# A two-layer RG-LRU and sparse-attention trunk on one core: convolution taps ordered ahead of the scans, and compressed values held as 128-row tiles

## The chip, the core and the metric

One core of a Trainium2 chip runs the whole program. The metric is the device time of one execution in microseconds (us), lower is better. The kernel before takes 1337.06 us (median of 3 runs, 1336.85 to 1337.19).

## What is computed

The input x is 512 tokens by 1024 channels in float32. Layer 0 is an RG-LRU block and a gated FFN, layer 1 is sparse attention (NSA) and a second gated FFN. Every sub-layer starts with an RMSNorm and ends with a residual add, and the trunk ends with a norm. The two parts that the change touches, cut from the reference:

```python
def rglru_mixer(x, w_in, conv_w, conv_b, gate_w, gate_b, a_param, w_out):
    y_br, x_br = jnp.split(x @ w_in, 2, axis=-1)          # 1280 channels each
    y_br = jax.nn.gelu(y_br)
    xc = causal_dwconv(x_br, conv_w, conv_b)              # 4 taps over time
    g = jnp.einsum('bsnc,gncd->gbsnd', xb, gate_w)        # 10 blocks of 128 x 128, two gates
    r_gate, i_gate = sigmoid(g + gate_b)
    log_a = -8 * r_gate * softplus(-a_param)
    bterm = sqrt(-expm1(2 * log_a)) * i_gate * xc
    h = scan of h[t] = exp(log_a)[t] * h[t-1] + bterm[t]
    return (h * y_br) @ w_out
...
# nsa_mixer, for each of 4 kv groups (4 heads each) and each block of queries
    p_cmp = masked_softmax(q k_cmp^T - alibi) * mask      # 31 compressed keys
    o_cmp = p_cmp @ v_cmp
...
    o = gate0 * o_cmp + gate1 * o_sel + gate2 * o_win
```

## The kernel before

**Layout.** Activations stand transposed, channels on the 128 partitions and 512 tokens along the free axis. A product in float32 is made as three matmuls in the fp32r format (`mm3`, L213 to L215): weight high part by data high part, high by low, low by high. So each weight tile that a DMA brings (`wraw`) is split by `_split`: ScalarE (ACT) copies its high part (`whi`, L184) and VectorE (DVE) subtracts for the low part (`wlo`, L185). `w()` wraps these splits in `high_priority(offset=HP)`, HP being 100, two weight tiles ahead of their use.

**Who orders the work.** Outside the attention core a scheduler of the tile framework orders each engine's instructions, by the order in the code, shifted by priorities, and by its own estimates. Inside the attention core (`tc.manual_schedule()`) the order is that of a table of steps in the code (`at(step, engine, f)`), the same for both kernels.

**The recurrent block** (`lru`, L402 on). Ten channel blocks n of 128 are worked through one after the other. For each: `project` makes `py[n]` and `px[n]` on TensorE (PE); `conv(n)` evacuates `px` with the norm's factor (`xr`, L424, DVE), starts `xc` on ACT (L426), adds three taps on DVE (L429, 128x511, 128x510, 128x509), and splits the result into `ch` (ACT, L433) and `cl` (DVE, L434); `gate_mm(n)` makes the two gates on PE from `ch` and `cl`; `gate_act(n)` is ACT's sigmoids and a POOL multiply (L466). The recurrence is made two blocks at a time (`burst`): exponentials, roots and GELUs on ACT, then for each block `back1` (DVE L482 and L484, POOL L483), `back2` (DVE L487, the scan L488, and a POOL multiply L489) and `back3` (`hh` on ACT L494, `hl` on DVE L495). `yev` evacuates `py` (L420, DVE). The output projection then reads `hh` and `hl` as its data, in chunks of eight blocks and then the last two.

**The attention core.** Scores of a unit (group g, 128 queries i, branch) are made by PE (L987, L988), reduced on DVE into one of NP = 10 buffers `P` (L1000), exponentiated on ACT, scaled on POOL (L1017), transposed on PE (L1041), split into `ph` (ACT) and `sq` (DVE L1050), and multiplied with the values `V2` on PE (L1057, L1062). The compressed branch's probabilities of group g stand in one tile of 128 rows, 32 rows for each query block i. The last key tile of a unit adds them with two matmuls (L1061) that use 32 rows of the array:

```python
cs_ = slice(32 * i, 32 * i + 32)
for pc in Pc[g]:
    T.matmul(po, Vc[cs_, g], pc[cs_], start=False, stop=False)
```

`Vc` (128 x 4 x 128) holds the compressed values with the same rows repeated for the four query blocks. It is written once by ACT (L863) and DVE (L864).

Of the kernel before, what the change touches and what calls it, by code (L numbers as in the profile page):

```python
# [10 lines left out]
F32 = mybir.dt.float32  # L11
F32R = mybir.dt.float32r
AF = mybir.ActivationFunctionType
ALU = mybir.AluOpType
# [3 lines left out]
NT = 512  # L18
# [7 lines left out]
WARM = 10  # L26
WLO, QLO, KLO, OLO = True, 'G', 'V', 'V'
KG = 3
NP = 10


UNITS = ((3, (0,)), (3, (1,)), (0, (0, 1)), (2, (0,)), (2, (1,)), (1, (0,)), (1, (1,)))
# [29 lines left out]
    ("o", 7, 114.23, 120.26),  # L62
)
HP = 100

START = {1: (1, 0), 3: (0, 1), 4: (1, 1)}
KA, DEF = 8, 5
# [4 lines left out]
P_CW, P_CB, P_GB, P_AP = 40, 80, 90, 110  # L72
# [28 lines left out]
class Trunk:  # L101
# [301 lines left out]
    def lru(self):  # L403
        S, V, G, T, prm = self.S, self.V, self.G, self.T, self.prm
        with ExitStack() as s:
# [3 lines left out]
            col = lambda c: prm[:, c:c + 1]  # L409
            py, px, pg = {}, {}, {}  # L410
            y, xc, xcs, r, ig, u, sq = {}, {}, {}, {}, {}, {}, {}
# [8 lines left out]
                V.tensor_mul(y[n], py[n], self.rbc)  # L420

            def conv(n):
                xr = p.tile([128, NT], F32, name="xr")
                V.tensor_mul(xr, px[n], self.rbc)  # L424
                xc[n] = p.tile([128, NT], F32, name="xc", bufs=3)
                S.activation(xc[n], xr, AF.Identity, scale=col(P_CW + 30 + n), bias=col(P_CB + n))  # L426
                for k in (2, 1, 0):
                    d = 3 - k
                    V.scalar_tensor_tensor(xc[n][:, d:], xr[:, :NT - d], col(P_CW + 10 * k + n),  # L429
                                           xc[n][:, d:], op0=ALU.mult, op1=ALU.add)  # L430
                ch = p.tile([128, NT], F32R, name="ch")
                cl = p.tile([128, NT], F32R, name="cl")
                S.activation(ch, xc[n], AF.Copy)  # L433
                V.tensor_sub(cl, xc[n], ch.bitcast(F32))  # L434
                xcs[n] = (ch, cl)
# [48 lines left out]
                V.tensor_mul(ig[n], ig[n], sq[n])  # L484

            def back2(n):
                V.scalar_tensor_tensor(ig[n], r[n], 1.0, ig[n], op0=ALU.add, op1=ALU.mult)  # L487
                V.tensor_tensor_scan(u[n], r[n], ig[n], 0.0, op0=ALU.mult, op1=ALU.add)  # L488
                self.G.tensor_mul(u[n], u[n], y[n])  # L489

# [76 lines left out]
            po = {}  # L567
# [106 lines left out]
    def nsa(self):  # L674
        S, V, G, T, prm, cst = self.S, self.V, self.G, self.T, self.prm, self.cst
        tc, a = self.tc, self.a
        with ExitStack() as s:
            kp = s.enter_context(tc.tile_pool(name="nsa_k", bufs=1))
# [2 lines left out]
            K2l = [kp.tile([128, 2, NT], F32R, name=f"K2l{g}") for g in range(4)]  # L681
            V2 = kp.tile([128, 4, 2, 4, 128], F32R, name="V2")
            Kc = kp.tile([128, 4, 32], F32, name="Kc")
            Vc = kp.tile([128, 4, 128], F32R, name="Vc")
            gtok = kp.tile([128, 4, 48], F32, name="gtok")
            Q = {}

# [70 lines left out]
            first = [project()]  # L758
# [3 lines left out]
            for kv in range(2):  # L762
                for j in range(2):
# [4 lines left out]
                    for gg in range(2):  # L768
                        b = 64 * gg
                        for par in range(2):  # L770
                            ob = 64 * par
                            for hf in range(2):
                                src = tv[b:b + 64, par::2, hf:hf + 31]
                                pc = P_POS + 32 * kv + 16 * par + 8 * hf
# [16 lines left out]
            for c in range(4):  # L791
                hi, lo = self.w()
                for kk in range(2):
                    k = 2 * c + kk
# [65 lines left out]
                    T.matmul(pk[:, 64 * g:64 * g + 64], hv4[:, m, g].rearrange("p r c -> p (r c)"),  # L860
                             w2[:, 256 + 128 * m:256 + 128 * m + 64], start=(m == 0), stop=(m == 1))
            pkv = pk[:, :256].rearrange("p (g d) -> p g d", g=4)
            S.activation(Vc[:, :, :64], pkv, AF.Copy)  # L863
            V.tensor_sub(Vc[:, :, 64:], pkv, Vc[:, :, :64].bitcast(F32))  # L864
            q_tile(1)
            cs.close()

# [165 lines left out]
            def values(u, steps):  # L1033
                g, i, br = u
# [17 lines left out]
                def pv(kt):  # L1052
                    if br == 0 and kt == 0:
                        Po[g, i] = newO()
                    po = Po[g, i]
                    last = br == 1 and kt == i
                    T.matmul(po, V2[:, kt, br, g], st["h", kt], start=(br == 0 and kt == 0), stop=False)  # L1057
                    if last:
                        cs_ = slice(32 * i, 32 * i + 32)
                        for pc in Pc[g]:  # L1060
                            T.matmul(po, Vc[cs_, g], pc[cs_], start=False, stop=False)  # L1061
                    T.matmul(po, V2[:, kt, br, g], st["l", kt], start=False, stop=last)  # L1062

                for kt in range(i + 1):
# [182 lines left out]
```

## Time and profile before

| what | value |
|---|---|
| median of 3 runs | 1337.06 us (1336.85 to 1337.19) |
| the profiled execution's own time | 1337.11 us |
| its span, first to last instruction | 1335.3 us |
| PE busy | 1309.2 us (98%), 6174 records |
| DVE busy | 790.4 us (59%) |
| ACT busy | 609.8 us (46%) |
| POOL busy | 251.7 us (19%) |
| chain that ended last | PE 88%, DVE 6%, ACT 2%, issue 2% |

The span starts with the recurrent block (to about 190 us), then the first FFN (to about 610 us), the attention layer (to about 910 us, its core from about 700) and the second FFN. A busy share is an average over these stages: DVE is busy 61.88 of the 69.2 us from 80 to 149.2 us.

### The profile page before, as it was taken

Reading aid. Unit: us, or ns where it says so; the run is one execution under the profiler, and the core shown is the slowest. Engines: PE = TensorE matmul, PEld = TensorE weight load, DVE = VectorE, ACT = ScalarE, POOL = GpSimd, SP = SyncE. Lnnn points to the kernel's source line nnn. Section 1 sums busy time; section 2 is a strip of 40 time slices with the busy share of each in tenths; the row PEclk is TensorE's granted clock in tenths of the full one; section 3 lists DMA queues with packets and bytes.
Section 4 is the critical chain, followed back from the end, with each engine's and each line's share of the span. In section 5 each row is a group of like instructions: output and inputs, shape, how many; then the busy total and the mean of one; then the engine's idle time right before and its main releaser. Section 6 shows DMA issues by size and latency. Waiting matters only on the chain.

```text
span 1335.3 us, 16299 instructions
## 1 busy us (share of the span) xinstructions
PE 1309.2 (98%) x6174; PEld 1064.8 (80%) x6174; DVE 790.4 (59%) x1260; ACT 609.8 (46%) x977; POOL 251.7 (19%) x260
## 2 busy tenths in 40 slices
PE   9989999999999999999999999999999999999997
PEld 7877787888888888887787787778888888888886
DVE  8798766555555533336357978876655555552223
ACT  5778844333333322221348878875433333332220
POOL 2222232000000001115007567643000000000110
PEclk9999999999999999999999999999999999999998
DMA  7222222232222222223231011013222222222221
GB/s 239 87 71 89 78 95 80 99 104 98 95 95 95 95 95 95 95 79 134 101 111 32 19 46 33 17 33 113 93 95 99 100 101 95 95 95 95 95 79 64
DMA packets 36223, 117.72 MB, mean 88 GB/s; under 512 B 4144, under 2 KB 7728, under 8 KB 36144
## 3 DMA queue, kind: packets, MB, share of 16 engines
q1 hardware_dynamic: 34848, 115.61, 25.5%
q8 instruction: 48, 0.79, 0.2%
q10 hardware_dynamic: 1296, 1.07, 0.2%
q14 instruction: 31, 0.25, 0.1%
HBM read 114.57 MB, written 2.10 MB: 87 GB/s over the span
## 4 chain that ended last, share of the span: by engine, by line
PE 88%; DVE 6%; issue 2%; ACT 2%; DMA 0%; POOL 0%; SPq 0%; POOLq 0%; DVEq 0%; ACTq 0%
PE bank L214 25%; PE bank L213 25%; PE bank L215 25%; PE bank L1041 2%; PE bank L1062 2%; PE bank L1057 1%; PE bank L987 1%; PE bank L988 1%; PE bank L839 1%; ACT L226 1%; PE bank L1061 1%; PE bank L800 1%; DVE u L488 1%; PE bank L801 1%; DVE xl L254 1%
## 5 line engine op out<-in xcount | busy, mean ns | idle before, releaser
L184 ACT ACTIVATE whi<-wraw 128x1024 fp32r<-128x1024 f32 x144 | 151.8, 1055 | 330.5 <-PE bank L214 282.3
L214 PE MATMUL bank<-xl,whi 128*128 128x512 f32 (+1 forms) x768 | 299.8, 390 | 2.4 <-DVE xl L254 2.3
L213 PE MATMUL bank<-xh,whi 128*128 128x512 f32 (+1 forms) x768 | 300.5, 392 | 0.5 <-DVE qn L726 0.2
L215 PE MATMUL bank<-xh,wlo 128*128 128x512 f32 (+1 forms) x768 | 299.4, 390 | 1.0 <-DVE wlo L185 0.5
L185 DVE TENSOR_TENSOR wlo<-wraw,whi 128x1024 fp32r<-128x1024 f32 x132 | 162.7, 1233 | 141.6 <-ACT whi L184 131.2
L264 POOL TENSOR_TENSOR ssum<-ssum,sq 128x512 f32<-128x512 f32 x27 | 44.9, 1663 | 789.5 <-issue 581.1
L214 PEld LDWEIGHTS bank<-xl,whi 128*128 128x128 f32 (+1 forms) x768 | 143.7, 187 | 34.1 <-DVE xl L254 4.6
L215 PEld LDWEIGHTS bank<-xh,wlo 128*128 128x128 f32 (+1 forms) x768 | 143.6, 187 | 32.7 <-DVE wlo L185 1.0
L213 PEld LDWEIGHTS bank<-xh,whi 128*128 128x128 f32 (+1 forms) x768 | 143.8, 187 | 31.2 <-DVE X L911 0.7
L184 ACT ACTIVATE whix<-wrawx 128x1024 fp32r<-128x1024 f32 x57 | 60.4, 1059 | 131.7 <-PE bank L214 122.4
L214 PE MATMUL bank<-xl,whix 128*128 128x512 f32 x296 | 117.0, 395 | 0.0
L213 PE MATMUL bank<-xh,whix 128*128 128x512 f32 x296 | 116.7, 394 | 0.0
L215 PE MATMUL bank<-xh,wlox 128*128 128x512 f32 x296 | 115.4, 390 | 0.0
L213 PE MATMUL bank<-fh,whi 128*128 128x512 f32 (+1 forms) x272 | 104.0, 382 | 0.0
L214 PE MATMUL bank<-fl,whi 128*128 128x512 f32 (+1 forms) x272 | 103.9, 382 | 0.0
L215 PE MATMUL bank<-fh,wlo 128*128 128x512 f32 (+1 forms) x272 | 103.8, 382 | 0.0
L185 DVE TENSOR_TENSOR wlox<-wrawx,whix 128x1024 fp32r<-128x1024 f32 x57 | 71.9, 1261 | 39.4 <-ACT whix L184 39.3
L621 DVE TENSOR_TENSOR ar<-bank,rbc 128x512 f32<-128x512 f32 x48 | 33.2, 691 | 99.5 <-PE bank L215 99.5
L1017 POOL TENSOR_SCALAR P<-P,c,gtok 128x512 f32<-128x512 f32 (+3 forms) x128 | 79.3, 634 | 45.3 <-DVE c L1013 34.5
L631 DVE TENSOR_TENSOR b<-bank,rbc 128x512 f32<-128x512 f32 x48 | 33.2, 691 | 86.2 <-PE bank L215 86.2
L226 ACT ACTIVATE P<-P,nm 128x512 f32<-128x512 f32 (+3 forms) x128 | 70.9, 556 | 15.1 <-DVE nm L1000 13.6
L226 ACT ACTIVATE t<-t 128x512 f32<-128x512 f32 x48 | 30.4, 632 | 98.0 <-DVE t L627 98.0
(217 smaller groups left out, 2326.2 us busy)
## 6 DMA issues: line engine op xcount, KB each, us to landing
wraw<-in_ffn_in_dram SPq DMA_DIRECT2D x65, 512.0 KB, 3.3
wraw<-in_ffn_out_dram SPq DMA_DIRECT2D x32, 512.0 KB, 3.3
wrawx<-in_ffn_in_dram SPq DMA_DIRECT2D x31, 512.0 KB, 3.3
wrawx<-in_ffn_out_dram SPq DMA_DIRECT2D x16, 512.0 KB, 3.2
wraw<-in_nsa_in_dram SPq DMA_DIRECT2D x16, 512.0 KB, 3.2
wraw<-in_lru_in_dram SPq DMA_DIRECT2D x12, 512.0 KB, 3.6
w<-in_cmp_w_dram SPq DMA_DIRECT2D x8, 512.0 KB, 4.6
wraw<-in_nsa_out_dram SPq DMA_DIRECT2D x8, 512.0 KB, 3.3
```

The lines of the kernel that those rows point to most:

```text
L184: self.S.activation(hi[:, c], raw[:, c], AF.Copy)
L185: (self.G.tensor_sub if self.manual and WLO else self.V.tensor_sub)(lo[:, c], raw[:, c], hi[:, c].bitcast(F32))
L213: mm(ps, wh, xh, start=first, stop=False)
L214: mm(ps, wh, xl, start=False, stop=False)
L215: mm(ps, wl, xh, start=False, stop=last)
L226: ins = self.S.activation(out, in_, func, **k)
L264: self.sq_eng.tensor_add(self.ssum, self.ssum, sq)
L621: V.tensor_mul(ar, pa, self.rbc)
L631: V.tensor_mul(b, pb, self.rbc)
L1017: G.tensor_scalar(Ps[g, i, br][r], Ps[g, i, br][r], st["c"][:, br, r:r + 1], gtok[:, i, gc:gc + 1], op0=ALU.mult, op1=ALU.mult)
L1041: T.transpose(st["t", kt][:, 128 * r:128 * r + 128], Ps[u][r][:, 128 * kt:128 * kt + 128], self.ident)
L1062: T.matmul(po, V2[:, kt, br, g], st["l", kt], start=False, stop=last)
```

## The change

In the recurrent block `conv(n)` now runs at a priority raised by 150 (CHP; the weight splits have 100), and the instruction L487 of `back2`, which stands ahead of the scan L488, may not be placed on DVE ahead of the last tap that was recorded so far (`self.tap`). That is an order on one engine without a semaphore.

In the attention layer `Vc` becomes 128 x 4 x 4 x 128: for each query block i a tile of 128 rows in which only rows 32i to 32i+31 are filled. POOL sets it to zero first, ACT and DVE fill it with four instructions each in place of one, and the two matmuls use all 128 rows with the whole tile `pc`. The zero rows add nothing, so the sums are the same. NP goes from 10 to 9.

```diff
-NP = 10
+NP = 9
...
+CHP = 150
...
             def conv(n):
+                with self.tc.high_priority(offset=CHP):
+                    conv_ops(n)
+
+            def conv_ops(n):
                 xr = p.tile([128, NT], F32, name="xr")
...
                 for k in (2, 1, 0):
                     d = 3 - k
-                    V.scalar_tensor_tensor(xc[n][:, d:], xr[:, :NT - d], col(P_CW + 10 * k + n),
-                                           xc[n][:, d:], op0=ALU.mult, op1=ALU.add)
+                    tap = V.scalar_tensor_tensor(xc[n][:, d:], xr[:, :NT - d], col(P_CW + 10 * k + n),
+                                                 xc[n][:, d:], op0=ALU.mult, op1=ALU.add)
+                self.tap = getattr(tap, "ins", tap).name
...
             def back2(n):
-                V.scalar_tensor_tensor(ig[n], r[n], 1.0, ig[n], op0=ALU.add, op1=ALU.mult)
+                ins = V.scalar_tensor_tensor(ig[n], r[n], 1.0, ig[n], op0=ALU.add, op1=ALU.mult)
+                self.tc.add_manual_dep(getattr(ins, "ins", ins), self.tap, mybir.DependencyInfo(
+                    mybir.DependencyClass.NoSync, mybir.DependencyReason.DATA), reason="taps first")
                 V.tensor_tensor_scan(u[n], r[n], ig[n], 0.0, op0=ALU.mult, op1=ALU.add)
...
-            Vc = kp.tile([128, 4, 128], F32R, name="Vc")
+            Vc = kp.tile([128, 4, 4, 128], F32R, name="Vc")
+            G.memset(Vc.bitcast(F32), 0.0)
...
-            S.activation(Vc[:, :, :64], pkv, AF.Copy)
-            V.tensor_sub(Vc[:, :, 64:], pkv, Vc[:, :, :64].bitcast(F32))
+            for i in range(4):
+                rs = slice(32 * i, 32 * i + 32)
+                S.activation(Vc[rs, i, :, :64], pkv[rs], AF.Copy)
+                V.tensor_sub(Vc[rs, i, :, 64:], pkv[rs], Vc[rs, i, :, :64].bitcast(F32))
...
-                        cs_ = slice(32 * i, 32 * i + 32)
                         for pc in Pc[g]:
-                            T.matmul(po, Vc[cs_, g], pc[cs_], start=False, stop=False)
+                            T.matmul(po, Vc[:, i, g], pc, start=False, stop=False)
```

The lines of the changed kernel are up to 14 higher: L424 is L430, L429 is L435, L434 is L441, L487 and L488 are L494 and L498, L495 is L505, L184 and L185 are L185 and L186, L226 is L227.

**DVE in the recurrent block, block 5's convolution.** These are VectorE's instructions behind `xr` of block 5 up to its `cl`. `hl_642` and `hl_749` are the recurrence's decay of blocks 2 and 3, `hh_919` is `y` of block 6. Before:

```order
L185 TENSOR_TENSOR wlox<-wrawx,whix 128x1024
L487 SCALAR_TENSOR_TENSOR ig<-hl_642,ig 128x512
L484 TENSOR_TENSOR ig<-ig,sqr 128x512
L429 SCALAR_TENSOR_TENSOR xc<-xr,prm,xc 128x511
L488 SCALAR_TENSOR_TENSOR u<-hl_642,ig 128x512
L429 SCALAR_TENSOR_TENSOR xc<-xr,prm,xc 128x510
L487 SCALAR_TENSOR_TENSOR ig<-hl_749,ig 128x512
L429 SCALAR_TENSOR_TENSOR xc<-xr,prm,xc 128x509
L488 SCALAR_TENSOR_TENSOR u<-hl_749,ig 128x512
L420 TENSOR_TENSOR hh_919<-bank_820,rbc 128x512
L185 TENSOR_TENSOR wlo<-wraw,whi 128x1024
L434 TENSOR_TENSOR cl<-xc,ch 128x512
```

The same place in the changed kernel:

```order
L186 TENSOR_TENSOR wlox<-wrawx,whix 128x1024
L489 SCALAR_TENSOR_TENSOR u<-hl_749,u 128x512
L491 TENSOR_TENSOR ig<-ig,sqr 128x512
L435 SCALAR_TENSOR_TENSOR xc<-xr,prm,xc 128x511
L435 SCALAR_TENSOR_TENSOR xc<-xr,prm,xc 128x510
L435 SCALAR_TENSOR_TENSOR xc<-xr,prm,xc 128x509
L494 SCALAR_TENSOR_TENSOR ig<-hl_642,ig 128x512
L498 SCALAR_TENSOR_TENSOR u<-hl_642,ig 128x512
L421 TENSOR_TENSOR hh_919<-bank_820,rbc 128x512
L441 TENSOR_TENSOR cl<-xc,ch 128x512
```

The three taps now follow each other, one pair of L487 and scan stays between them and `cl`, the pair of block 3 has gone behind the next block's taps, and a weight split has gone behind `cl`. `xr` itself has moved ahead of `back1` of block 3, whose L482 (L489 now) stood ahead of it.

**ACT at the end of the recurrent block.** This is ScalarE from the last gate's sigmoid (`hl_1308`, block 9) to the roots (`sqr`) of the last burst; the exponentials are `hl_1271` and `hl_1308` from themselves. Before:

```order
L226 ACTIVATE hl_1308<-bank_1300,prm 128x512
L184 ACTIVATE whix<-wrawx 128x1024
L226 ACTIVATE ig<-bank_1304,prm 128x512
L226 ACTIVATE u<-hl_1308,sp 128x512
L226 ACT_TABLE_LOAD
L226 ACTIVATE hl_1271<-hl_1271,sp 128x512
L184 ACTIVATE whi<-wraw 128x1024
L226 ACTIVATE hl_1308<-hl_1308,sp 128x512
L226 ACT_TABLE_LOAD
L226 ACTIVATE sqr<-u 128x512 x2
L184 ACTIVATE whi<-wraw 128x1024
L226 ACT_TABLE_LOAD
```

In the changed kernel:

```order
L227 ACTIVATE hl_1308<-bank_1300,prm 128x512
L504 ACTIVATE hh_1296<-u 128x512
L227 ACTIVATE ig<-bank_1304,prm 128x512
L227 ACTIVATE u<-hl_1308,sp 128x512
L185 ACTIVATE whix<-wrawx 128x1024
L185 ACTIVATE whi<-wraw 128x1024
L227 ACT_TABLE_LOAD
L227 ACTIVATE hl_1271<-hl_1271,sp 128x512
L227 ACTIVATE hl_1308<-hl_1308,sp 128x512
L227 ACT_TABLE_LOAD
L227 ACTIVATE sqr<-u 128x512
L185 ACTIVATE whi<-wraw 128x1024
```

`hh` of block 7 (`hh_1296`) has moved in between the two gates' sigmoids, and a weight split now stands between the two roots, ahead of the second.

**POOL at the start of the attention layer.** `ssum` is the norm's sum over the residual that the first FFN leaves. In the changed kernel:

```order
L265 TENSOR_TENSOR ssum<-ssum,sq 128x512 x7
L279 TENSOR_TENSOR rtok<-nv,mhalf 128x4
L265 TENSOR_TENSOR ssum<-ssum,sq 128x512 x6
L696 MEMSET Vc 128x2048
L265 TENSOR_TENSOR ssum<-ssum,sq 128x512
L279 TENSOR_TENSOR rtok<-nv,mhalf 128x4
```

The zeroing stands ahead of the last of seven adds; before, the seven followed each other.

## Rows read from the trace of the kernel before

**Rows 1.** The first line of the page: the span.

```profile
span 1335.3 us, 16299 instructions
```

**Rows 2.** Who PE waited for over the whole span: us in total, number of waits, longest us. Two rows of twelve, the two largest.

```profile
PE bank L214 <- DVE cl L434: 4.7, 2, 3.0
PE bank L213 <- ACT ch L433: 3.7, 2, 2.6
```

**Rows 3.** Stretches of the span: its length, then the busy time (and instructions, those that reach in counted) of PE, PEld, DVE, ACT and POOL, the mean granted TensorE clock, DMA share and GB/s.

```profile
80.00:149.20 69.20, 63.25 (x266) 50.55 (x265) 61.88 (x73) 57.60 (x76) 19.19 (x16) 0.98 0.25 82
95.80:104.70 8.90, 4.82 (x13) 3.27 (x12) 8.86 (x13) 6.82 (x10) 1.61 (x2) 0.81 0.24 74
127.00:129.70 2.70, 0.97 (x5) 0.49 (x3) 2.70 (x4) 2.27 (x3) 0.38 (x1) 1.00 0.11 23
149.20:156.00 6.80, 4.17 (x11) 2.71 (x10) 6.39 (x6) 2.75 (x4) 2.64 (x2) 0.75 0.01 4
700.00:905.00 205.00, 201.66 (x1187) 155.96 (x1188) 166.24 (x490) 163.28 (x413) 131.54 (x171) 1.00 0.09 31
```

**Rows 4.** DVE in order of time around block 5's convolution: start us, length us, line, operation, tiles, shapes.

```profile
86.57 1.10 DVE L482 SCALAR_TENSOR_TENSOR u<-hl,u 128x512 f32<-128x512 f32 x1
87.59 0.68 DVE L424 TENSOR_TENSOR xr<-bank,rbc 128x512 f32<-128x512 f32 x1
...
89.37 0.68 DVE L487 SCALAR_TENSOR_TENSOR ig<-hl,ig 128x512 f32<-128x512 f32 x1
...
90.57 1.77 DVE L429 SCALAR_TENSOR_TENSOR xc<-xr,prm,xc 128x511 f32<-128x511 f32 x1
92.27 1.21 DVE L488 TENSOR_TENSOR_SCAN u<-hl,ig 128x512 f32<-128x512 f32 x1
93.40 0.72 DVE L429 SCALAR_TENSOR_TENSOR xc<-xr,prm,xc 128x510 f32<-128x510 f32 x1
94.05 1.78 DVE L487 SCALAR_TENSOR_TENSOR ig<-hl,ig 128x512 f32<-128x512 f32 x1
95.75 0.74 DVE L429 SCALAR_TENSOR_TENSOR xc<-xr,prm,xc 128x509 f32<-128x509 f32 x1
96.41 1.21 DVE L488 TENSOR_TENSOR_SCAN u<-hl,ig 128x512 f32<-128x512 f32 x1
...
98.13 1.98 DVE L185 TENSOR_TENSOR wlo<-wraw,whi 128x1024 fp32r<-128x1024 f32 x1
100.03 0.68 DVE L434 TENSOR_TENSOR cl<-xc,ch 128x512 fp32r<-128x512 f32 x1
```

**Rows 5.** POOL in the same stretch, the same columns and behind them the idle time before and what ended it.

```profile
90.16 1.64 POOL L466 TENSOR_TENSOR ig<-ig,xc 128x512 f32<-128x512 f32 x1 [1.78 <-ACT ig L226]
93.63 1.65 POOL L489 TENSOR_TENSOR u<-u,hh 128x512 f32<-128x512 f32 x1 [1.83 <-DVE u L488]
```

**Rows 6.** The end of the recurrent block: the last `hl` on DVE, and PE's first matmul that reads it, in order of time.

```profile
176.49 0.68 DVE L495 TENSOR_TENSOR hl<-u,hh 128x512 fp32r<-128x512 f32 x1
177.51 0.40 PE L214 MATMUL bank<-hl,whi 128*128 128x512 f32 x1
```

**Rows 7.** PE in order of time around one pair of 32-row matmuls: start us, length us, line, tiles, rows and columns of the array, data.

```profile
726.62 0.39 PE L1057 MATMUL bank<-ph,V 128*128 128x512 f32 x1
726.94 0.50 PE L1061 MATMUL bank<-ch,Vc 32*128 32x512 f32 x1
727.28 0.39 PE L1061 MATMUL bank<-cl,Vc 32*128 32x512 f32 x1
727.61 0.50 PE L1062 MATMUL bank<-sq,V 128*128 128x512 f32 x1
727.94 0.40 PE L213 MATMUL bank<-xh,whi 128*128 128x512 f32 x1
728.18 0.40 PE L214 MATMUL bank<-xl,whi 128*128 128x512 f32 x1
728.41 0.39 PE L215 MATMUL bank<-xh,wlo 128*128 128x512 f32 x1
```

**Rows 8.** All 32-row matmuls that read `ch`, as one group: count, then busy us, mean ns, idle us before.

```profile
L1061 PE MATMUL bank<-ch,Vc 32*128 32x512 f32 x16 | 7.9, 494 | 0.0
```

**Rows 9.** The first use of a tenth `P` buffer (DVE, 714.46) beside the last transposes that read the first one (PE, 715.12), and the same for the twentieth and the eleventh (735.89 and 736.17).

```profile
714.46 0.28 DVE L1000 CUSTOM_DVE_ANT_0 P<-bank,cst 128x128 f32<-128x128 f32 x1
715.12 0.60 PE L1041 MATMUL bank<-cst,P 128*128 128x128 f32 x4
735.89 0.41 DVE L1000 CUSTOM_DVE_ANT_0 P<-bank,cst 128x256 f32<-128x256 f32 x1
736.17 0.60 PE L1041 MATMUL bank<-cst,P 128*128 128x128 f32 x4
```

**Rows 10.** The writing of `Vc` on ACT and DVE with the next instruction of each, and POOL's last add of the norm ahead of the attention layer.

```profile
689.39 0.39 ACT L863 ACTIVATE Vc<-bank 128x256 fp32r<-128x256 f32 x1
694.38 1.06 ACT L184 ACTIVATE whi<-wraw 128x1024 fp32r<-128x1024 f32 x1 [4.60 <-issue]
690.90 0.43 DVE L864 TENSOR_TENSOR Vc<-bank,Vc 128x256 fp32r<-128x256 f32 x1
694.56 0.75 DVE L699 SCALAR_TENSOR_TENSOR qn<-bank,cst,rbc 128x512 f32<-128x512 f32 x1 [3.23 <-PE bank L215]
605.47 1.29 POOL L264 TENSOR_TENSOR ssum<-ssum,sq 128x512 f32<-128x512 f32 x1 [14.88 <-ACT sq L263]
```

## The prediction, made before the changed kernel ran

> **What bounds the kernel now.** I read the page first, then who PE waited for, then stretches of the span, then single engines in order of time. The page puts PE busy for nearly all of the 1335.3 us [rows 1] and the chain that ended last mostly on PE, so the time changes only where PE idles or where a matmul costs more than it needs to. The list of PE's waits shows the two largest: 4.7 us for DVE's `cl` and 3.7 us for ACT's `ch` [rows 2], both made by the convolution of the recurrent block and read by the gates' matmuls. The stretches show three such gates and what each costs [rows 3]. A full-width matmul of 512 columns takes 0.235 us from start to start (727.94 to 728.41 is two of them [rows 7]). In 95.8 to 104.7 twelve matmuls start, which would be 2.8 of 8.9 us: 6.1 lost. In 127.0 to 129.7 three start: 2.0 lost. In 149.2 to 156.0 ten start: 4.4 lost. In the first and the third the granted clock averages 0.81 and 0.75 of its 2.4 GHz: behind the idle time PE ran for some us at 1.2 GHz, and that is part of the loss. DVE is busy 8.86 of 8.9, 2.70 of 2.70 and 6.39 of 6.80 us there: PE waits for DVE's queue, not for a transfer. In the attention core PE is busy 201.66 of 205 us, so there a matmul's own cost counts.
>
> **Gates one and two, in the recurrent block.** For block 5, DVE needs from 87.59 (`xr`) to 100.71 (end of `cl`) [rows 4]. Start to start, what the change takes out of this stretch is: L487 0.60, scan 1.13, L487 1.70, scan 1.14, and the split L185 behind the taps 1.90: 6.5 us. Put in are `back1` of block 3, whose L482 took 1.02 ahead of `xr`, and one pair of L487 and scan, 0.60 and 1.13: 2.7 us. So `cl` comes 3.7 us sooner after `xr`, and `xr` itself 1.0 us sooner, since that L482 no longer stands ahead of it: 4.7 us. PE's idle time at the first gate is 8.90 less 4.82, 4.1 us, at the second 2.70 less 0.97, 1.7 us [rows 3]; both are less than 4.7, so I take both losses away whole, with the low clock behind the first: **-8.1 us**. The nearest bound on the other side: two DVE instructions of rows 4 are long because they stand beside a POOL multiply (L429 1.77 where its neighbours take 0.72 to 0.74, beside L466 of 1.64; L487 1.78, beside L489 [rows 5]). POOL's L466 is due when the taps run, now as before; if all three taps were to meet POOL, `cl` would come up to 2 us later than reckoned, and of the first gate's idle 2 us and some of its low clock would stay: -4 instead of -8.1.
>
> **Gate three.** Here I expect no gain. From 80 to 149.2 us DVE is busy 61.88 of 69.2 us [rows 3]: 7.3 us idle. The change takes no work off DVE; if PE comes 8.1 us sooner to the third gate, DVE has used up its idle time and is itself the bound. What it saves is the one split and the pairs that now follow `cl`, what it lacks is the lead, and I set the two equal: 0, between -4.4 (the whole loss gone) and +2.
>
> **The tail, what is late next.** The last `hl` ends at 177.17 and PE reads it at 177.51 [rows 6]: 0.34 us to spare. Whatever lengthens the way from the third gate to it becomes a new wait. On ACT an `hh` now stands between the sigmoids, and a weight split ahead of the second root; a split is 1.06 us [rows 10], and an `hh` waits for a scan and a POOL multiply (1.21 and 1.65 [rows 4, 5]). I take two splits' worth less the 0.34: **+1.8 us**, from 0 (the extra pieces fit into gaps of ACT) to 4 (both, and the `hh` blocks the sigmoids for a scan and a multiply). The recurrent block: -8.1 + 0 + 1.8 = -6.3 us.
>
> **128-row compressed values.** Around a pair of 32-row matmuls PE goes from the start of L1057 (726.62) to that of the matmul after L1062 (727.94) in 1.32 us for four matmuls [rows 7]; four full-width ones take 0.94. Each boundary, and the pair itself, costs about 0.1 more than usual, though all have 512 columns. There are 16 such pairs [rows 8]: 16 x 0.38 = 6.1 us, all on PE's path in a core where PE has 3.3 us idle in 205. With 128 rows and the same 512 columns I take the ordinary 0.235: **-6.1 us**. It could be less by what ACT and DVE, busy 80% there, then fail to deliver: down to -4.
>
> **Nine `P` buffers.** The reduction that takes the tenth buffer started at 714.46, while the transposes that free the first run from 715.12; with nine buffers it waits about 0.9 us, since the first of four, 0.27 us long, must end. The twentieth waits 0.5 us in the same way (735.89 against 736.17) [rows 9]. DVE stands still for that time, and behind it the splits that PE waits for. PE may see all of it or nothing: 0 to 1.5, taken as **+0.3 us**, since PE's list has hardly a wait there.
>
> **The rest.** Writing `Vc` in four pieces, each at most as long as the whole (0.39 and 0.43 us), adds at most 1.2 us on ACT and 1.3 on DVE; both idle behind it, for 4.60 and 3.23 us [rows 10], so 0. The zeroing on POOL stands ahead of the norm's last add, which starts at 605.47 after 14.88 us of idle. No row has a fill of that size; it writes four times what that add writes, which took 1.29, so at most 5.2 us and at least nothing. The idle time covers it; if it were released only at the end of that gap, the norm would be up to 5 us late and PE with it.
>
> **Sum.** -6.3 - 6.1 + 0.3 = -12.1 us, from -16.5 (gate three gone too, the rest as reckoned) to -6 (gates one and two and the matmuls at their weak ends, the rest as reckoned). The profiled execution took 1337.11 us with a span of 1335.3, and the median of the runs is 1337.06, the same within 0.1. So the span becomes 1323.2 and the time **1325.0 us**; its own range is 1320.5 to 1331.
>
> **The rivals.**
> *The recurrent block gives nothing.* DVE is the bound and the waits move from the gates to the output projection: the 8.1 us come back in the tail, where only 0.34 us were spare. For it: DVE's 90% share. Against: 7.3 us of its idle time lie ahead of the third gate, and it has to do no more than before. Time: 1337.1 - 5.8 = 1331.3. Chance 0.09.
> *The 32-row form is not the cause.* The slow boundaries come from something that stays (the accumulation into one bank). Against: the steps stand exactly where the row count changes and between the two 32-row matmuls, and from 727.94 on the starts are back at 0.235 [rows 7]. Time: 1337.1 - 6.3 + 0.3 = 1331.1. Chance 0.05.
> *Small arrays run side by side.* Four strips of 32 rows make up the array. If small matmuls ran side by side on them, the pair would be the cheap form: at best a quarter of 0.235 each, 0.12 us a pair against 0.47 with 128 rows, 16 x 0.35 = +5.6 us, and 1337.1 - 6.3 + 0.3 + 5.6 = 1336.7. The trace speaks against it: the pair's starts are 0.34 and 0.33 apart [rows 7], longer than full-width ones. Chance 0.02. The Trainium skill, page "TensorEngine Tiling (Array Packing)", section "Theoretical Speedup", gives up to four times for a dimension of 32 or less, which would bring this rival about; its section "Key Properties" also says that a change of tiling mode drains the engine, and the trace agrees with that one (0.1 us at each boundary).
> *The ring of nine binds: slower.* Place: L1000 on DVE, in the windows in which the unit being multiplied, the one ready and the one being scored hold ten buffers (a group's units hold 4, 4, 2, 4, 4, 2, 2, so five windows of seven, 20 in four groups). Two of them are shown late already, by 0.9 and 0.5 us [rows 9]; if DVE, once late, stays late, each makes PE wait. From 0.75 us a unit on (20 x 0.75 = 15) the gain is gone and the kernel is slower; at 1.0 us a unit it is 1337.1 - 12.4 + 20 = 1344.7. Against: PE drains the transposes in its fixed order whether DVE is late or not, so a delay does not add up. Chance 0.03.
>
> **Chances.** Forecast 0.81, the others as named. 1320.5 to 1331.5 holds the forecast's own range and the two rivals at 1331; outside lie the rivals at 1336.7 and 1344.7 and the ends of the forecast's terms, together under 2 in 10. What a measurement of this kernel tells from no change is about 0.2%, 2.7 us. Faster 0.94 (the forecast nearly whole and the first two rivals), the same 0.03, slower 0.03.
>
> **What would show it.** Right: PE's list of waits has no gate of block 5 or 7, one of block 9 stays with a stretch at the low clock, a new wait of 1 to 2 us stands before the last two blocks' output projection; L1074 shows 128 rows and 0.235 us to the next start. Wrong: `ch` or `cl` still the longest waits at three gates; a wait of several us at the output projection; PE waits for `nm` (L1014) more than the few now; a wait at the norm near 605.

## The result, and the profile after

The changed kernel takes 1326.77 us (median of 5 runs, 1325.63 to 1328.08), against 1337.19 for the kernel before on the same chip: ratio 0.992, 95% interval 0.9905 to 0.9933. The forecast was 1325.0. The profiled run took 1326.77 us too, so its trace stands for the median. Its span and PE's waits, the rows that answer to [rows 1] and [rows 2]:

```profile
span 1325.0 us, 16294 instructions
...
PE bank L1001 <- DVE nm L1014: 2.4, 3, 1.3
PE bank L215 <- DVE xl L255: 2.0, 3, 1.1
PE bank L214 <- ACT ch L440: 1.5, 1, 1.5
...
PE bank L215 <- DVE cl L441: 0.8, 1, 0.8
PE bank L214 <- ACT hh L504: 0.8, 1, 0.8
```

`cl` and `ch` stood at 8.4 us in four waits; 2.3 us in two are left, both at block 9. DVE around block 5's convolution, as in [rows 4]:

```profile
88.14 3.55 DVE L435 SCALAR_TENSOR_TENSOR xc<-xr,prm,xc 128x511 f32<-128x511 f32 x3
91.61 0.68 DVE L494 SCALAR_TENSOR_TENSOR ig<-hl,ig 128x512 f32<-128x512 f32 x1
92.33 1.23 DVE L498 TENSOR_TENSOR_SCAN u<-hl,ig 128x512 f32<-128x512 f32 x1
93.47 0.67 DVE L421 TENSOR_TENSOR hh<-bank,rbc 128x512 f32<-128x512 f32 x1
94.06 1.49 DVE L441 TENSOR_TENSOR cl<-xc,ch 128x512 fp32r<-128x512 f32 x1
95.47 1.21 DVE L186 TENSOR_TENSOR wlo<-wraw,whi 128x1024 fp32r<-128x1024 f32 x1
```

The three taps stand in one piece and `cl` is done at 95.55 in place of 100.71. PE reads `ch` at 95.74 and `cl` at 95.97, without idle time. One pair of matmuls of the compressed values, which answers to [rows 7]:

```profile
721.16 0.40 PE L1071 MATMUL bank<-ph,V 128*128 128x512 f32 x1
721.39 0.40 PE L1074 MATMUL bank<-ch,Vc 128*128 128x512 f32 x1
721.63 0.40 PE L1074 MATMUL bank<-cl,Vc 128*128 128x512 f32 x1
721.87 0.39 PE L1075 MATMUL bank<-sq,V 128*128 128x512 f32 x1
722.10 0.40 PE L214 MATMUL bank<-xh,whi 128*128 128x512 f32 x1
```

From 721.16 to 722.10 it is 0.94 us, against 1.32 before. Stretches of the changed kernel, with the columns of [rows 3]: the first gate, the third gate, the attention core, and the first FFN's start.

```profile
87.30:96.30 9.00, 9.00 (x41) 7.42 (x41) 8.89 (x10) 7.54 (x12) 3.82 (x3) 1.00 0.18 58
...
139.50:151.00 11.50, 9.25 (x32) 6.31 (x31) 7.97 (x9) 7.63 (x11) 4.67 (x4) 0.85 0.01 2
...
700.00:905.00 205.00, 202.30 (x1212) 163.86 (x1212) 169.42 (x492) 164.35 (x413) 131.59 (x171) 1.00 0.11 34
...
205.10:208.60 3.50, 3.50 (x10) 2.74 (x10) 1.30 (x2) 0.14 (x1) 1.95 (x1) 0.51 0.30 77
```

Read the last row: at the first FFN's start PE makes 10 matmuls in 3.5 us, at 1.2 GHz (a granted clock of 0.51). The same stretch of the kernel before:

```profile
212.30:215.80 3.50, 3.50 (x17) 2.87 (x17) 1.31 (x2) 0.14 (x1) 1.95 (x1) 1.00 0.28 74
```

17 matmuls at 2.4 GHz: 7 x 0.235 = 1.6 us are lost here in the changed kernel. Both kernels idle 1.06 to 1.07 us for `xl` just ahead, the changed one first, then the one before:

```profile
203.64 0.50 PE L215 MATMUL bank<-xl,whi 128*128 128x512 f32 x1 [1.06 <-DVE xl L255]
...
210.85 0.50 PE L214 MATMUL bank<-xl,whi 128*128 128x512 f32 x1 [1.07 <-DVE xl L254]
```

PE makes the same matmuls in nearly the same order in both kernels, so one can compare when the same matmul starts. This table gives, for the profiled run of each kernel (the experiments too), the start less that of the kernel before, in us; negative is earlier.

| kernel | behind gate two | behind the first read of the last `hh` | behind the FFN's first norm | ahead of the core | behind the core |
|---|---|---|---|---|---|
| start before | 129.93 | 177.98 | 214.62 | 710.98 | 913.26 |
| changed | -8.54 | -7.20 | -5.63 | -5.68 | -10.54 |
| convolution alone | -8.57 | -4.60 | -4.62 | -4.65 | -4.69 |
| tie alone | -8.62 | -6.20 | -6.19 | -6.03 | -6.08 |
| priority alone | -1.23 | +0.21 | +0.16 | +0.21 | +0.21 |
| `Vc` and nine buffers alone | +1.17 | +1.58 | +1.56 | +1.50 | -3.28 |
| nine buffers alone | +0.26 | +0.40 | +0.41 | +0.60 | +0.88 |
| 64 rows | +0.02 | +0.16 | +0.17 | +1.20 | +1.18 |
| products on DVE | -8.56 | -8.73 | -8.76 | -8.39 | -13.13 |
| and gate product | -8.56 | -10.73 | -9.48 | -9.14 | -13.95 |
| changed, norm filled | -8.35 | -7.09 | -7.10 | -6.62 | -11.36 |
| all three | -8.50 | -10.65 | -10.63 | -9.64 | -14.47 |
| exponentials first | -8.42 | -8.09 | -6.51 | -6.27 | -10.98 |

The three largest steps between the norm and the core (1.03 us with 64 rows, 0.99 with all three, 0.48 with the norm filled) stand at one group of matmuls (L839 before). PE waits there for the DMA of the compression's weights, 0.9, 0.8 and 0.3 us in these runs; in the kernel before and the changed one it does not.

### The profile page after: what moved, and what is told of

Read it like the earlier page. It is cut to its first block, busy times and chain, and to the rows that moved or that the text cites. A ratio compares the mean times of both kernels' runs of the same rounds, so it can differ in the third digit from the quotient of the medians.

```text
span 1325.0 us, 16294 instructions
## 1 busy us (share of the span) xinstructions
PE 1303.2 (98%) x6174; PEld 1066.6 (80%) x6174; DVE 786.9 (59%) x1263; ACT 611.0 (46%) x980; POOL 252.0 (19%) x261
## 3 DMA queue, kind: packets, MB, share of 16 engines
q10 hardware_dynamic: 1296, 1.07, 0.2%
## 4 chain that ended last, share of the span: by engine, by line
PE 90%; DVE 5%; ACT 2%; issue 2%; POOL 1%; DMA 0%; SPq 0%; POOLq 0%; DVEq 0%; ACTq 0%
PE bank L215 26%; PE bank L214 26%; PE bank L216 26%; PE bank L1055 2%; PE bank L1075 1%; PE bank L1071 1%; PE bank L1001 1%; PE bank L851 1%; PE bank L1002 1%; PE bank L812 1%; ACT P L227 1%; PE bank L811 1%; PE bank L813 1%; DVE xl L255 1%; DVE xc L435 1%
## 5 line engine op out<-in xcount | busy, mean ns | idle before, releaser
L185 ACT ACTIVATE whi<-wraw 128x1024 fp32r<-128x1024 f32 x144 | 151.8, 1055 | 328.3 <-PE bank L215 284.9
L186 DVE TENSOR_TENSOR wlo<-wraw,whi 128x1024 fp32r<-128x1024 f32 x132 | 161.4, 1223 | 139.7 <-ACT whi L185 127.8
L185 ACT ACTIVATE whix<-wrawx 128x1024 fp32r<-128x1024 f32 x57 | 60.4, 1060 | 130.1 <-PE bank L215 120.5
L186 DVE TENSOR_TENSOR wlox<-wrawx,whix 128x1024 fp32r<-128x1024 f32 x57 | 70.8, 1241 | 38.7 <-ACT whix L185 38.5
L227 ACT ACTIVATE P<-P,nm 128x512 f32<-128x512 f32 (+3 forms) x128 | 70.9, 556 | 16.3 <-DVE nm L1014 15.8
L227 ACT ACTIVATE t<-t 128x512 f32<-128x512 f32 x48 | 30.3, 632 | 98.0 <-DVE t L637 98.0
```

What stands on the lines that cost most here:

```text
L185: self.S.activation(hi[:, c], raw[:, c], AF.Copy)
L186: (self.G.tensor_sub if self.manual and WLO else self.V.tensor_sub)(lo[:, c], raw[:, c], hi[:, c].bitcast(F32))
L227: ins = self.S.activation(out, in_, func, **k)
```

## The experiments

Ratios are to the runs of the kernel before on the same chip, with their 95% interval; a gain in us is the difference of the medians, where nothing else is said.

**Which half gives what.** *The convolution alone* (`Vc` and NP as before):

> The kernel before with the convolution's priority and tie alone (Vc in 32-row form, ten P buffers). Theory: the gain of the recurrent block stands by itself. PE's starts are 8.4 us earlier behind the second gate and 7.2 us earlier at the output projection, as in the changed kernel, and nothing later takes it back: 1337.2 - 7.2 = 1330.0 us; if the low granted clock behind the 1.06 us of idle at the first FFN's start comes here too (it cost 1.6 us in the changed kernel), 1331.6. Rival, the recurrent block gives nothing (its gain comes back at the output projection): 1337.2.

Measured: 1332.38 us (1329.67 to 1332.89), ratio 0.9955 (0.9942 to 0.9967): -5.9 us. The gain stands by itself, and the rival that it gives nothing falls. Two of its five runs took the expected 1329.67 and 1330.21 us, three 1332.38 to 1332.89, the profiled one among them. In it PE's starts behind gate two are the expected ones, at the last `hh` they are not: -4.60, not -7.2. On every engine the order up to there is that of the changed kernel; what differs is the third gate. POOL, DVE and ACT there, in order of time, in the changed kernel:

```profile
143.61 1.55 POOL L499 TENSOR_TENSOR u<-u,hh 128x512 f32<-128x512 f32 x1 [3.84 <-DVE u L498]
...
143.94 2.29 DVE L498 TENSOR_TENSOR_SCAN u<-hl,ig 128x512 f32<-128x512 f32 x1
...
145.18 0.63 ACT L504 ACTIVATE hh<-u 128x512 fp32r<-128x512 f32 x1 [2.84 <-POOL u L499]
```

and with the convolution alone (POOL's row merges two products, of which the first takes 2.61 us):

```profile
143.57 3.84 POOL L499 TENSOR_TENSOR u<-u,hh 128x512 f32<-128x512 f32 x2 [3.84 <-DVE u L498]
...
143.90 1.22 DVE L498 TENSOR_TENSOR_SCAN u<-hl,ig 128x512 f32<-128x512 f32 x1
...
146.22 0.63 ACT L504 ACTIVATE hh<-u 128x512 fp32r<-128x512 f32 x1 [3.90 <-POOL u L499]
```

In both the product starts 0.33 us ahead of the scan. Once the scan takes 2.29 us, about as long as it would by waiting for the product; once it takes its usual 1.22, and the product's result comes 1.0 us later. The Trainium skill, page "SBUF — State Buffer", section "Who interferes with whom", says that a DVE instruction with two SBUF inputs contends with a GpSimd instruction that reads SBUF, and that the order of issue decides which of the two is blocked. The rows agree that one waits for the other; they do not agree that the earlier start, as the profile gives it, decides. Behind that, PE waited 1.7 us for `hh` of block 6 and then ran at a granted clock of 0.50 from 148.7 to 152.1 us. In the changed kernel's run the low clock came sooner, from 143.7 to 147.1, partly under the waits.

*`Vc` in 128 rows and nine buffers alone*:

> The kernel before with the 128-row Vc and nine P buffers alone. Theory: 16 pairs cost 0.94 us in place of 1.33 with their neighbours, -6.3 us, and about 1 us of it comes back as waits for DVE in the core: 1337.2 - 5.3 = 1331.9 us. Rival, the 32-row form is not the cause: 1337.2 or a little above. Rival, the two halves of the change help or hinder each other: then the gains of this run and of the convolution alone don't add up to the 10.4 us of both.

Measured: 1333.51 us (1333.00 to 1334.21), ratio 0.9969 (0.9957 to 0.998): -4.7 us. Over the core PE gains 4.8 us (table), at the 16 places of such a pair, four starts each as in [rows 7], 6.26: from 21.28 to 15.02 us, as in the changed kernel. -5.9 and -4.7 add up to -10.6, the whole change gave -10.4. So the halves neither help nor hinder each other by more than the intervals, some 1.5 us each, would hide.

*Nine buffers alone* (`NP = 9`):

> The kernel before with nine P buffers in place of ten, nothing else. Theory: the two late reductions (0.9 and 0.5 us on DVE) reach PE at most once each: +0.5 us (0 to +1.5), 1337.7. Rival, the ring binds in five windows of seven: +15 to +20 us, 1352 to 1357. If it is 0, what came back in the core of the changed kernel (about 1 us) has another cause than the ring.

Measured: 1337.80 us, ratio 1.0001 (0.9992 to 1.001). The rival falls. Over the core PE loses 0.28 us, 0.24 of it in one step, at a group of transposes (L1041, at 724.80 before); of the 1.4 us that come back in the core of the changed kernel (6.26 - 4.86) the ring is 0.24.

**Why the 32-row pair was dear.** *64 rows*, ten buffers; `Vc` is zeroed and block i fills its 32 rows of tile i % 2:

```diff
-            Vc = kp.tile([128, 4, 128], F32R, name="Vc")
+            Vc = kp.tile([128, 2, 4, 128], F32R, name="Vc")
...
-                        cs_ = slice(32 * i, 32 * i + 32)
+                        cs_ = slice(64 * (i // 2), 64 * (i // 2) + 64)
                         for pc in Pc[g]:
-                            T.matmul(po, Vc[cs_, g], pc[cs_], start=False, stop=False)
+                            T.matmul(po, Vc[cs_, i % 2, g], pc[cs_], start=False, stop=False)
```

> The kernel before with Vc as two tiles whose halves of 64 rows are zero but for 32, so that the 32 matmuls use 64 rows of the array; ten P buffers stay. Theory, the cost is that of going from the full array to a part of it and back: it stays whole, 1337.2 us (within 0.5), and the places cost 1.3 us each. Rival, the cost goes with the rows that are missing (a weight load or data of fewer partitions): about half, -3 us, 1334. Rival, it belongs to 32 rows alone: -6.3 us, 1331.

Measured: 1337.85 us, ratio 1.0002 (0.9993 to 1.001). One place of its trace:

```profile
727.82 0.39 PE L1061 MATMUL bank<-ph,V 128*128 128x512 f32 x1
728.14 0.49 PE L1065 MATMUL bank<-ch,Vc 64*128 64x512 f32 x1
728.47 0.38 PE L1065 MATMUL bank<-cl,Vc 64*128 64x512 f32 x1
728.79 0.50 PE L1066 MATMUL bank<-sq,V 128*128 128x512 f32 x1
729.12 0.40 PE L213 MATMUL bank<-xh,whi 128*128 128x512 f32 x1
```

1.30 us, the steps of [rows 7] one by one; all 16 places take 21.31 us (32 rows: 21.28). So the number of missing rows costs nothing, and the change between the whole array and a part of it costs all of it. Of the four late starts only two are at such a change, into the pair and out of it. What happens there stands in the weight loads (PEld) of the kernel before, for the matmuls of [rows 7] at 726.94, 727.28, 727.61 and 727.94:

```profile
726.94 0.18 PEld L1061 LDWEIGHTS bank<-ch,Vc 32*128 32x128 f32 x1 [0.30 <-issue]
727.05 0.18 PEld L1061 LDWEIGHTS bank<-cl,Vc 32*128 32x128 f32 x1
727.60 0.19 PEld L1062 LDWEIGHTS bank<-sq,V 128*128 128x128 f32 x1 [0.37 <-DVE nm L1000]
727.71 0.19 PEld L213 LDWEIGHTS bank<-xh,whi 128*128 128x128 f32 x1
```

The second and the fourth start 0.23 us ahead of their matmul, under the one before; the first and the third, at the changes, start together with it, and those two matmuls are recorded 0.50 us long in place of 0.39. It is so at all 16 places with 32 and with 64 rows; with 128 rows the loads of `ch` and `sq` lead by 0.19 to 0.24 us as well. Two uncovered loads of 0.18 and 0.19 us are, by my estimate, nearly all of the 0.39 us that a place loses. The Trainium skill, page "TensorEngine Tiling (Array Packing)", section "Key Properties", which the prediction cited, says that changing the tiling mode drains TensorE. The rows agree: at both changes the next load waits.

**Tie or priority.** *Priority alone*, and *tie alone* (L487 behind the last tap, priority as before):

> The kernel before with the convolution's priority of 150 alone, no tie of L487 to the taps. On DVE the taps of block 5 still have the two pairs of L487 and scan among them; only cl has moved ahead of one weight split (1.9 us). Theory, the tie does the work: of the 4.1 us of idle at the first gate 1.9 go, little else: 1338.2 - 2 = 1336 us (1335 to 1338). Rival, the priority does it: about 1332, like the convolution's whole change alone.

> The kernel before with the tie alone, priority as before. DVE's taps follow each other as in the changed kernel, PE's order is that of the changed kernel, and only ch and cl stand behind a weight split again (1.0 and 1.2 us). Theory: those splits are covered by what the gates had to spare, 1332.4 us like the convolution's whole change alone, up to 2 more. Rival, tie and priority each give half: 1335.

Measured: priority alone 1335.77 us, ratio 0.9989 (0.998 to 0.9998); tie alone 1331.55, ratio 0.9953 (0.994 to 0.9965). The tie gives the whole gain, the priority by itself 1.5 us by the ratio; in its profiled run even that was gone behind the third gate (table). That run took 1337.31 us, where six of the eleven took 1335.23 to 1335.77, and at the first gate the low clock lasted 6.8 us in it, against 3.4 in the kernel before. Its trace keeps the first gate's two waits, that for `cl` shorter than the 3.0 of [rows 2]:

```profile
97.68 0.50 PE L214 MATMUL bank<-ch,ghi 128*128 128x512 f32 x1 [1.73 <-ACT ch L440]
100.06 0.79 PE L215 MATMUL bank<-cl,ghi 128*128 128x512 f32 x1 [1.88 <-DVE cl L441]
```

In the tie's run POOL and DVE met at the third gate as with the convolution alone (PE waited 1.7 us for `hh`), but no stretch of the recurrent block ran at the low clock. So the last `hh` is reached at -7.20 (changed), -6.20 (tie alone) and -4.60 us (convolution alone), by which of the two engines went first and by where the low clock fell. The first and the last have the same order on every engine up to there; the tie's differs from it in a few weight splits and one `xr`, on DVE and ACT alone.

**What is left at the third gate and in the tail.** *The products by `y` of blocks 6 to 9 on DVE*, then also *the gate products of blocks 8 and 9* (L473, input gate times convolution):

```diff
-                self.G.tensor_mul(u[n], u[n], y[n])
+                (V if n >= 6 else self.G).tensor_mul(u[n], u[n], y[n])
...
-                self.G.tensor_mul(ig[n], ig[n], xc[n])
+                (V if n >= 8 else self.G).tensor_mul(ig[n], ig[n], xc[n])
```

> The changed kernel with the product by y (L499, POOL, 1.3 to 2.1 us) of blocks 6 to 9 made on DVE (about 0.7 us each). Theory: at the third gate POOL's product and DVE's scan stand in each other's way (the scan took 2.29 us in one run, the product 2.6 in another, 1.2 and 1.3 when alone); without that hh of block 6 comes by 145.4 us in every run, and the last hh 1.5 us sooner, so the waits of 0.8 and 0.2 us at the last two blocks' output projection go. 1326.8 - 1 to 2.5 = 1325 us, and the runs spread less. Rival, DVE is the bound at the third gate and four more products of 0.7 us make PE wait longer there: 1327 to 1329.

> As the one with the products of blocks 6 to 9 on DVE, and the product of gate and convolution (L473, POOL, 1.6 us) of blocks 8 and 9 on DVE too. In the changed kernel L473 of block 8 runs at 138.17 beside the three taps of block 9, which take 3.55 us in place of some 2.1. Theory: the taps end 0.7 us or more earlier, although DVE has a product more, PE's wait for ch at the third gate falls from 1.5 to under 1 us and the wait for cl and the low clock behind them get less: 2 to 4 us under the changed kernel, 1323 to 1325. Rival, DVE's own work is the bound: no better than with the products of blocks 6 to 9 alone.

Measured: 1325.02 us (1324.31 to 1326.25), ratio 0.9906 (0.9893 to 0.992), and 1323.50 (1321.72 to 1323.72), ratio 0.989 (0.9875 to 0.9905), where the changed kernel has 0.9919. The steps in the table are clearer than the times: at the last `hh` 1.5 us and 3.5 us sooner than the changed kernel's run. In the first the wait for the last `hh` fell only from 0.77 to 0.17 us; that for `hl` stayed at 0.23; the other 0.9 us came at the third gate. That its run had no low clock in the recurrent block is not the reason: the run with the norm filled, of the changed kernel's order there, had none either and is at -7.09. The taps of block 9 and their `cl` in the changed kernel, with POOL's product beside the taps:

```profile
137.55 3.55 DVE L435 SCALAR_TENSOR_TENSOR xc<-xr,prm,xc 128x511 f32<-128x511 f32 x3
...
143.35 0.67 DVE L441 TENSOR_TENSOR cl<-xc,ch 128x512 fp32r<-128x512 f32 x1
...
138.17 1.60 POOL L473 TENSOR_TENSOR ig<-ig,xc 128x512 f32<-128x512 f32 x1
```

and with that product on DVE, and PE's one wait left at the gate:

```profile
137.50 1.07 DVE L435 SCALAR_TENSOR_TENSOR xc<-xr,prm,xc 128x511 f32<-128x511 f32 x1
138.49 0.68 DVE L473 TENSOR_TENSOR ig<-ig,xc 128x512 f32<-128x512 f32 x1
139.10 1.52 DVE L435 SCALAR_TENSOR_TENSOR xc<-xr,prm,xc 128x510 f32<-128x510 f32 x2
...
141.74 0.68 DVE L441 TENSOR_TENSOR cl<-xc,ch 128x512 fp32r<-128x512 f32 x1
...
141.40 0.73 PE L214 MATMUL bank<-ch,ghi 128*128 128x512 f32 x2 [1.02 <-ACT ch L440]
```

With a product more on its queue DVE ends the taps at 140.6 in place of 141.1. And `cl` has moved ahead of the scan that it followed in the changed kernel (L498 at 142.22 there, at 142.34 here), so it comes 1.6 us sooner, and PE no longer waits for it. So at the third gate it was not DVE's amount of work that bound, but its meetings with POOL and its order; no run tells the shares of these two, and what makes the 1.0 us that is left stays open.

*Exponentials and roots of the last burst ahead of the weight splits* (a priority of 250 for them, in the changed kernel):

> The changed kernel with the exponentials and roots of the last burst at a priority of 250, so that on ACT they stand ahead of the weight splits (two of them now stand ahead of the exponentials and one between the roots; the first waits until PE has read the old weights). Theory, the tail's wait for the last hh is that queue on ACT: with three splits of 1.05 us behind the roots, the waits of 0.8 and 0.2 us at the last two blocks' output projection are gone, whatever the third gate does; a wait of up to 1 us for the late weights (wlox) may come ahead of them. Net 0 to -1 us against the changed kernel. Rival, the tail is bound by DVE and POOL behind the roots: the waits stay.

Measured: 1325.73 us in two runs, ratio 0.991 (0.9882 to 0.9939): the time can't tell. The trace can. ACT in the changed kernel, from the split that waits for PE to the last `hh`:

```profile
150.07 1.06 ACT L185 ACTIVATE whix<-wrawx 128x1024 fp32r<-128x1024 f32 x1 [0.26 <-PE bank L215]
151.03 1.04 ACT L185 ACTIVATE whi<-wraw 128x1024 fp32r<-128x1024 f32 x1
...
153.39 1.34 ACT L227 ACTIVATE hl<-hl,sp 128x512 f32<-128x512 f32 x2
...
156.60 1.06 ACT L185 ACTIVATE whi<-wraw 128x1024 fp32r<-128x1024 f32 x1
...
168.80 0.63 ACT L504 ACTIVATE hh<-u 128x512 fp32r<-128x512 f32 x1 [3.21 <-POOL u L499]
```

With the splits behind the roots the exponentials start at 151.26, the last `hh` at 167.62, and neither of the waits of 0.77 and 0.23 us is left; in their place PE waits 0.30 us for `wlox`. The same matmul starts 0.9 us sooner than in the changed kernel. The tail's wait was ACT's queue, and behind its first split PE itself: where PE is late at the third gate, that split is late too, and all that follows. So the tail costs the same 1.5 us in the changed kernel, the tie and the convolution alone, whatever the third gate cost before it.

**The low clock at the first FFN's start.** *Four more matmuls of 512 columns* in the idle time there; the next group's first matmul overwrites their result.

```diff
+FILLS = 4
...
+                    self.T.matmul(pa, hi[:, c7], xh, start=False, stop=False)
+                    pb = newacc()
+                    for _ in range(FILLS):
+                        self.T.matmul(pb, hi[:, c7], xh, start=True, stop=True)
+                    self.T.matmul(pa, hi[:, c7], xl, start=False, stop=False)
...
```

> The changed kernel with four more matmuls of 512 columns (0.23 us each) in the 1.06 us that PE idles at the first FFN's start; their result is overwritten by the next group's first matmul. Theory: the 1.6 us that the changed kernel's profiled run lost there came from the low granted clock behind that idle, and the idle is the cause: with it filled, no run has the low clock there, PE's starts behind it are 2.4 us apart for ten matmuls as in the runs without it, and the median falls by 0 to 1.6 us, 1325 to 1327. Rival, the low clock there has another cause (the eight one-column matmuls of the norm, or the waits ahead): it still comes in some runs, and the median stays.

Measured: 1326.29 us (1325.75 to 1326.60), ratio 0.991 (0.9895 to 0.9924). The fill (L632) and what follows, in the trace and as a stretch:

```profile
202.53 1.07 PE L632 MATMUL bank<-xh,whi 128*128 128x512 f32 x4
203.77 0.50 PE L633 MATMUL bank<-xl,whi 128*128 128x512 f32 x1 [0.17 <-DVE xl L256]
...
205.20:208.70 3.50, 3.50 (x17) 2.90 (x18) 1.31 (x2) 0.16 (x1) 1.95 (x1) 1.00 0.31 87
```

17 matmuls in 3.5 us, full clock, and no step in the table between the last `hh` and the norm (-7.09, -7.10). But without the fill the low clock is there in three profiled runs (changed, gate product, exponentials first) and absent in eight with the same idle, so two filled runs without it are what one would often see by chance; and the median fell by less than its interval. That this idle brings the low clock on is likely, not shown.

*All three together* (both products and the fill):

> The changed kernel with the products of blocks 6 to 9 and the gate products of blocks 8 and 9 on DVE, and the four filling matmuls at the first FFN's start. Theory: the gains add up, since the one at the FFN's start is the low clock that the profiled run without the filling had there (1.3 us): 1323.5 - 0 to 1.6 = 1322 to 1323. Rival, the low clock then falls elsewhere (the third gate's idle of 1.0 us): 1323.5.

Measured: 1322.61 us (1322.43 to 1323.10), ratio 0.9883 (0.9866 to 0.9899), the fastest of all, 0.4% under the changed kernel by the ratios (0.9883 and 0.9919), whose intervals do not overlap.

## Why the prediction was right, point by point

Forecast -12.1 us, measured -10.3 in the spans (1335.3 to 1325.0) and -10.4 in the medians. By the starts of the profiled run:

| term | predicted | measured |
|---|---|---|
| gates one and two | -8.1 | -8.54 |
| gate three | 0 (-4.4 to +2) | -0.18 |
| tail | +1.8 (0 to 4) | +1.52 |
| first FFN's start | no term | +1.57 |
| 16 pairs | -6.1 | -6.26 |
| nine buffers | +0.3 (0 to 1.5) | +0.24 (that run alone) |
| other waits in the core | no term | +1.2 |
| sum | -12.1 | -10.5 |

- **Gates one and two** went whole, and for the reason given. The bound named beside it half came true: the taps meet L473 (POOL, 1.60 us from 88.77) and take 3.55 us, 1.4 more than three of 0.72; what was to spare covered it.
- **Gate three** gave nothing, as forecast, but the reason was wrong in part: not DVE's amount of work, since it did more in the run with the gate product and was sooner. And 0 was in part the luck of that run: from gate two to the matmuls behind the third gate and its low clock, the run with the norm filled, of the same order, came out at -0.3, but the tie alone lost 0.9 us and the convolution alone, of the same order too, 2.4.
- **The tail** was right in size and in its place on ACT, with a split between the roots; that the first split waits for PE, and so hands on PE's delay, I had not seen.
- **The pairs** cost and gain what [rows 7] gave; the 64-row run shows the cause. The prediction spoke of 0.1 us at each boundary; only two of the four boundaries are a change of rows, and at each of these a weight load of 0.18 to 0.19 us stands uncovered.
- **Left out, the first FFN's start.** The sum took the clock into account where a stretch of the trace before showed it, and nowhere else. The same idle was there in the trace before, and the low clock came to it only now. An idle of about 1 us ahead of full work needed a bound of its own: 0 to 1.6 us.
- **Too small, the waits in the core.** I gave the ring alone a term. PE, faster by 6 us over the core, comes sooner to what DVE makes: the largest step is 0.36 us at L1001, which waits for `nm`, and 0.16 at L1075, which waits for `sq`; the ring's run has neither. No run has 128 rows with ten buffers, but the trace of the changed kernel speaks against the ring here: beyond its waits in the kernel before, DVE waits for a buffer at 709.85 and 730.36 alone (1.02 and 0.23 us), and ahead of the step at L1001 (744.73) it stands still for PE, up to 734.84, and then works almost without a pause. The rest are starts 0.1 us later each, whose cause stays open.

Of the rivals, the recurrent block giving nothing and the ring binding are refuted by the runs of each alone, the 32-row form not being the cause by the 16 places, and small arrays side by side by the same places, where the pair was the dearer form. The two matmuls of a pair use the same 32 rows, so this tells nothing of matmuls on different strips.

## What to carry to other kernels

Where one engine waits at a few places for a queue, tie the work that nobody waits for behind the work that is waited for: a tie on the instruction gave the whole gain here, a priority 1.5 of 6 us. A few matmuls of 32 or 64 rows among full ones cost at each change, 0.39 us a pair here; with rows of zeros up to 128 that cost was gone. Behind an idle of about 1 us on TensorE that both kernels have, 1.2 to 1.6 us were lost to the low clock in three profiled runs and nothing in eight: such an idle, also one that stays, needs a bound in the sum.

## What the runs showed of the chip

- The program order being the same up to there (but for the few splits and the `xr` in the tie's run), who goes first of a POOL product and a DVE scan that start 0.33 us apart changes from run to run: the product in three profiled runs (changed, norm filled, exponentials first), the scan in two (convolution alone, tie alone), by 1.0 us for what waits on the product.
- Where the low clock falls, and how long it stays, differs between runs of the same order. In the run of `Vc` alone, whose recurrent block is that of the kernel before, it stayed from 100.1 to 106.9 us, where in the kernel before it was back at full from 104.8, and the block ended 1.6 us later:

```profile
100.10:106.90 6.80, 6.13 (x14) 4.81 (x15) 6.73 (x10) 6.50 (x8) 1.43 (x1) 0.50 0.50 166
```

```profile
104.80:108.20 3.40, 3.40 (x16) 2.77 (x15) 2.29 (x2) 2.09 (x3) 1.00 (x1) 1.00 0.42 154
```

(first the run of `Vc` alone, then the kernel before).
- 64 rows of the array cost as much as 32: 1.33 us a place, 0.94 with all 128. A weight load of another row count than the matmul ahead of it started together with its own matmul at all 32 changes of the kernel before and all 32 of the 64-row run; one of the same row count mostly started 0.23 us ahead.
